# The scan of a state-space layer: splitting weights and summing squares on GpSimd instead of VectorE

## The chip, the cores and the metric

The program runs on one core of a Trainium2 chip. A core has a matrix engine (TensorE, PE in the rows), three engines for elementwise work (VectorE or DVE, ScalarE or ACT, GpSimd or POOL), and SyncE (SP), which here only issues transfers between HBM and the on-chip memory SBUF. Matmul results land in PSUM, which GpSimd cannot read. Each engine works off its own list of instructions strictly in order and waits for the others by semaphores. The metric is the device time of one execution in microseconds (us), lower is better.

## The reference, cut to what matters

```python
def reference(x, ...):
    x = first_block(x, ...)      # layer 1: RG-LRU and latent attention; layer 2: a state-space layer (SSD)
    return second_block(x, ...)  # short convolution, stick-breaking attention, MLP, gate

def _ssd_layer(x, w_in, conv_w, ...):            # layer 2, the one that the change touches
    z, xbc, dt = split(x @ w_in)                 # 1024 rows of sequence, 2048 + 3072 + 32 columns
    xs, bm, cm = split(silu(causal_conv(xbc)))   # 32 heads of 64; 4 groups with a state of 128
    for c in range(8):                           # chunks of 128 rows, one after the other
        decay = exp(cs_l - cs_s) where l >= s else 0       # cs: cumulative sum of dt * a
        y_diag = ((C_c @ B_c.T) * decay) @ (xs * dt)
        y_off  = (C_c @ state) * exp(cs)
        state  = state * exp(cs_end) + B_c.T @ (xs * dt * exp(cs_end - cs))
    y = (y_diag + y_off + d_skip * xs) * silu(z)
    y = y * rsqrt(mean(y * y over each group of 512 channels) + 1e-6)
    return (y * norm_w) @ w_out
...
```

Everything is float32.

## The kernel before, in words

Activations lie transposed in SBUF, channels on the 128 partitions and the sequence of 1024 along the free dimension. To keep float32 accuracy in a faster matmul format, each operand is split into a leading part (`hi`, rounded by ScalarE in a copy) and a trailing part (`lo`, the difference, made by the helper `lo` in line 260). `mm3` (lines 189, 193 and 194) then issues three matmuls for each product: hi·hi, lo·hi and hi·lo.

`weights` streams a weight block: for each four tiles of 128x128 it issues a DMA into `wr` (L179), ScalarE rounds it into `wh` (L180), and an engine subtracts to give `wl` (L260). Each of the three names has three buffers, so TensorE is fed two blocks ahead at most. The engine that makes `wl` is `self.weng`: GpSimd at the start, VectorE from the head of `phase_b` on, GpSimd again from `finish_b` on.

`phase_b` is layer 2. Its loop goes through 32 steps `(u, c)`: `u` is one of eight half groups of four heads, `c` one of four pairs of chunks. `stage1` loads the decay table into `L` (one buffer; L907), ScalarE turns it into exponentials (L911, L913), VectorE masks it (L916), and both operands `Xf` and `L` are split into `Xh`, `Xl`, `Lh`, `Ll`; it also advances the state (`hs`, `hh`, `hl`). `stage2` multiplies (`poff`, `pd` in the PSUM names `u` and `w`), adds up on VectorE in `et` (L971 to L988), multiplies by the gate in `zt` (L991), squares on ScalarE (L997) and adds the squares into `acc2` (L999, L1002). After two chunk pairs of a group's second half, a matmul with ones (L1007) sums `acc2` over the partitions, ScalarE takes the root and SyncE stores the row `rsd` (L1009). Between the steps, projections for later steps are slipped in (`conv_silu`, `proj_z`), and when these are used up, parts of the output projection (`part`), for which `y_act` loads the normalised `y` into the buffers `XH` and `XL` that the layer's input has left.

Where a group ends (every eighth step) the next group's `B` and `C` have to be prepared first (`prep_bc`), and only then can `stage1` go on.

The order on each engine isn't the order of the code: a scheduler sorts the recorded instructions by its own simulated times. So a small edit can move rows on every engine.

Of the kernel before, what the change touches and what calls it, by code (L numbers as in the profile page):

```python
# [12 lines left out]
A = mybir.AluOpType  # L13
# [36 lines left out]
class K:  # L50
# [38 lines left out]
    def v(self, name, i=0, n=1):  # L89
        o, _ = VEC[name]  # L90
        return self.vec[:, o + i:o + i + n]
# [5 lines left out]
    def P(self, nm, w=T):  # L97
        return self.ap.tile([128, w], F32, tag="P", bufs=self.ns, name=self.nm(nm))
# [650 lines left out]
    def phase_b(self):  # L749
        nc, v, P, R, cp, d = self.nc, self.v, self.P, self.R, self.cp, self.d  # L750
# [9 lines left out]


        first = self.first
        self.weng = nc.vector
        ps = first.pop(0)
        H = slice(0, 32)
        dt, e, cs = P("dt"), P("e"), P("cs")
# [53 lines left out]
        bc, xs, acc2 = {}, {}, {}  # L820
# [124 lines left out]
        def stage2(u, cpair):  # L945
            g, hg = divmod(u, 2)
            h0 = 8 * g + 4 * hg
            c0 = 2 * cpair
            th, tl, ch, cl, cbm = bc[g]
            xt = xs[u]  # L950
            Xh, Xl, Lh, Ll, prev = stg.pop((u, cpair))
            cols = slice(c0 * 128, c0 * 128 + 256)

            poff = self.u1()
            for c in range(2):
                if prev[c]:
                    hh, hl = prev[c]
                    s = slice((c0 + c) * 128, (c0 + c) * 128 + 128)
                    for p in range(2):
                        q = slice(p * 128, p * 128 + 128)  # L960
                        self.mm3(poff[:, c * 256 + p * 128:c * 256 + p * 128 + 128], (hh[:, q], hl[:, q]), (ch[:, s], cl[:, s]), True, True)
            et = self.E("et")
            ev = et.rearrange("p (c q l) -> p c q l", c=2, q=2)
            for j in range(2):
                for p in range(2):
                    nc.sync.dma_start(ev[64 * j:64 * j + 64, :, p, :], ecd[c0:c0 + 2, h0 + 2 * p + j, :].partition_broadcast(64))
            zt = self.E("zt")
            zv = zt.rearrange("p (q x) -> p q x", q=2)
            nc.sync.dma_start(zv, self.zd[u * 256:u * 256 + 256, cols].rearrange("(q p) x -> p q x", q=2))
            if c0:  # L970
                nc.vector.tensor_tensor(et, et, poff, op=A.mult)  # L971
            else:
                nc.vector.memset(et[:, 0:256], 0.0)
                nc.vector.tensor_tensor(et[:, 256:], et[:, 256:], poff[:, 256:], op=A.mult)
            for p in range(2):
                nc.vector.scalar_tensor_tensor(ev[:, :, p, :], xt[p][:, cols].rearrange("p (c l) -> p c l", c=2), v("d_skip", 4 * g + 2 * hg + p),
                                               ev[:, :, p, :], op0=A.mult, op1=A.add)

            for c in range(2):
                pd = self.u1()  # L980
                for p in range(2):
                    q = slice(c * 256 + p * 128, c * 256 + p * 128 + 128)
                    s = slice(c * HN + p * 256, c * HN + p * 256 + 256)
                    self.mm3(pd[:, p * 256:p * 256 + 256], (Xh[:, q], Xl[:, q]), (Lh[:, s], Ll[:, s]), True, True)
                pv = pd.rearrange("p (q j l) -> p q j l", q=2, j=2)
                for j in range(2):
                    r = slice(64 * j, 64 * j + 64)
                    nc.vector.tensor_tensor(ev[r, c], ev[r, c], pv[r, :, j, :], op=A.add)  # L988
            for p in range(2):
                z = zv[:, p, :].rearrange("p (c l) -> p c l", c=2)  # L990
                nc.vector.scalar_tensor_tensor(z, ev[:, :, p, :], 0.5, z, op0=A.mult, op1=A.mult)  # L991
            nc.sync.dma_start(self.yd[u * 256:u * 256 + 256, cols].rearrange("(q p) x -> p q x", q=2), zv)

            if g not in acc2:
                acc2[g] = P("acc2")
            sq = et
            nc.scalar.activation(sq, zt, AF.Square)  # L997
            if hg == 0:
                nc.vector.tensor_tensor(acc2[g][:, cols], sq[:, 0:256], sq[:, 256:], op=A.add)  # L999
            else:  # L1000
                for p in range(2):
                    nc.vector.tensor_tensor(acc2[g][:, cols], acc2[g][:, cols], sq[:, p * 256:p * 256 + 256], op=A.add)  # L1002
                if cpair % 2:
                    n = cpair // 2
                    s = slice(n * HN, n * HN + HN)
                    ps = self.u1()
                    nc.tensor.matmul(ps, self.ones, acc2[g][:, s], start=True, stop=True)  # L1007
                    self.rstd_from(acc2[g][:, s], ps, 1.0 / 512, 1e-6)
                    nc.sync.dma_start(self.rsd[g:g + 1, s], acc2[g][0:1, s])  # L1009
# [36 lines left out]
        for j, (u, c) in enumerate(steps):  # L1046
            last = c == 3 and u % 2
            if j + 1 < len(steps) and not last:
                stage1(*steps[j + 1])
            stage2(u, c)  # L1050
            if c == 2 and u % 2 and u < 7:
                load_bc(u // 2 + 1)
            if last and u < 7:
                prep_bc(u // 2 + 1)
                stage1(*steps[j + 1])
            if act:
                left = len(steps) - j
                for i in range(-(-len(parts) // left)):
                    part(parts.pop(0))
            elif u < 7:  # L1060
                project(PATTERN[j % len(PATTERN)])
                if not any(queue.values()):
                    for k in range(8):
                        act.append(self.y_act(k, self.XH[k], self.XL[k]))
# [864 lines left out]
```

## Time and profile before

| | us |
|---|---|
| median of 3 runs | 2759.99 |
| lowest, highest run | 2750.53, 2760.86 |
| the profiled execution's own time | 2749.49 |
| its span (first to last instruction) | 2747.7 |
| TensorE, VectorE, ScalarE, GpSimd busy | 2590.2, 1933.3, 1438.8, 655.1 |

The mean granted clock of TensorE is 0.975 of full speed. Busy times of different engines overlap, so they don't add up to the span; what counts in a stretch is which engine the others wait for. `phase_b` and the head of `finish_b` lie at 546 to 1276 us.

### The profile page before, as it was taken

What the parts mean: (1) busy time and instruction counts of PE and PEld (TensorE: products, weight loads), DVE (VectorE), ACT (ScalarE), POOL (GpSimd) and SP (SyncE); (2) the same over time, 40 slices, a digit from 0 to 9 for tenths busy, and PEclk for the clock granted to TensorE, in tenths of its full rate; (3) what the DMA queues carried; (4) which work ended last, traced back from release to release, by engine and by line L of the source; (5) the groups of instructions that cost most, each with busy time, mean ns of one, the idle gap of its engine ahead of it and who ended that gap; (6) DMA issues with size and microseconds to landing.
All of it is one profiled execution on the core that took longest, in us unless ns stands there. A gap on an engine that the chain in (4) does not pass through costs nothing. (4 is left out here: it accounts for less than half of the span.)

```text
span 2747.7 us, 34501 instructions
## 1 busy us (share of the span) xinstructions
PE 2590.2 (94%) x12000; PEld 2077.2 (76%) x12000; DVE 1933.3 (70%) x2754; ACT 1438.8 (52%) x2447; POOL 655.1 (24%) x467
## 2 busy tenths in 40 slices
PE   8999999999989899789989999998899999999997
PEld 6777887787877788677767776766688888887786
DVE  5683766769978698785575215889696666777577
ACT  5553754656656555543463224665665455443465
POOL 2642754400000000004455324566300000000024
PEclk9999999999999999889999999999999999999999
DMA  4444533443434344366443334543454446977324
GB/s 128 159 159 142 139 93 108 151 133 115 139 103 134 113 125 138 94 217 221 141 133 92 125 130 123 159 118 98 161 207 148 148 152 222 336 245 238 120 72 152
DMA packets 214419, 407.14 MB, mean 148 GB/s; under 512 B 22636, under 2 KB 61548, under 8 KB 214244
## 3 DMA queue, kind: packets, MB, share of 16 engines
q1 hardware_dynamic: 214244, 404.93, 45.9%
q8 instruction: 94, 1.54, 0.2%
q14 instruction: 81, 0.66, 0.1%
HBM read 297.35 MB, written 107.50 MB: 147 GB/s over the span
## 5 line engine op out<-in xcount | busy, mean ns | idle before, releaser
L260 POOL TENSOR_TENSOR wl<-wr,wh 128x512 fp32r<-128x512 f32 (+2 forms) x262 | 371.5, 1422 | 1158.4 <-ACT wh L180 1105.3
L189 PE MATMUL g<-XH,wh 128*128 128x512 f32 x1296 | 525.3, 406 | 23.8 <-ACT xc L812 10.3
L193 PE MATMUL g<-XL,wh 128*128 128x512 f32 x1296 | 523.7, 404 | 4.6 <-DVE XL L746 2.4
L194 PE MATMUL g<-XH,wl 128*128 128x512 f32 x1296 | 521.1, 402 | 4.7 <-POOL wl L260 4.7
L180 ACT CAST wh<-wr 128x512 fp32r<-128x512 f32 (+2 forms) x367 | 221.0, 604 | 395.5 <-PE g L193 164.8
L189 PEld LDWEIGHTS g<-XH,wh 128*128 128x128 f32 x1296 | 248.3, 192 | 85.1 <-ACT xc L812 11.3
L193 PEld LDWEIGHTS g<-XL,wh 128*128 128x128 f32 x1296 | 248.2, 192 | 65.4 <-DVE XL L260 4.4
L194 PEld LDWEIGHTS g<-XH,wl 128*128 128x128 f32 x1296 | 248.1, 191 | 64.8 <-POOL wl L260 6.3
L260 DVE TENSOR_TENSOR wl<-wr,wh 128x512 fp32r<-128x512 f32 (+1 forms) x198 | 133.0, 683 | 75.4 <-ACT wh L1531 45.0
L260 POOL TENSOR_TENSOR yl<-yl,yh 128x1024 fp32r<-128x1024 f32 x4 | 9.6, 2400 | 715.0 <-ACT yh L1075 712.3
L193 PE MATMUL m<-XL,XH 128*128 128x512 f32 x368 | 144.8, 393 | 5.5 <-DVE XL L260 5.5
L189 PE MATMUL m<-XH,XH 128*128 128x512 f32 x368 | 143.7, 392 | 0.0
L194 PE MATMUL m<-XH,XL 128*128 128x512 f32 x368 | 143.6, 392 | 0.0
L911 ACT ACTIVATE L<-L,tm 128x128 f32<-128x128 f32 x256 | 78.8, 389 | 122.4 <-DMA L<-csd 116.4
L194 PE MATMUL t<-XH,wl 128*128 128x512 f32 (+1 forms) x328 | 129.4, 395 | 1.3 <-POOL wl L260 1.2
L189 PE MATMUL t<-XH,wh 128*128 128x512 f32 (+1 forms) x328 | 128.2, 391 | 1.0 <-ACT wh L180 1.0
L193 PE MATMUL t<-XL,wh 128*128 128x512 f32 (+1 forms) x328 | 128.5, 392 | 0.0
L1615 ACT CAST XH<-a 128x1024 fp32r<-128x1024 f32 x46 | 48.2, 1049 | 134.6 <-PE m L193 109.3
L1283 DVE TENSOR_TENSOR_SCAN kp<-kp,zero 128x640 f32<-128x640 f32 (+5 forms) x64 | 107.0, 1693 | 5.5 <-ACT kp L1279 3.8
L1284 POOL TENSOR_TENSOR sg<-sg,kp 128x639 f32<-128x639 f32 (+5 forms) x64 | 91.3, 1436 | 75.5 <-DVE kp L1283 71.9
L577 ACT CAST XL<-t 128x512 fp32r<-128x512 f32 (+2 forms) x192 | 78.4, 426 | 46.1 <-DVE XL L260 21.2
L260 DVE TENSOR_TENSOR XL<-t,XL 128x512 fp32r<-128x512 f32 (+2 forms) x192 | 87.5, 472 | 14.8 <-ACT XL L577 14.0
(584 smaller groups left out, 6519.4 us busy)
## 6 DMA issues: line engine op xcount, KB each, us to landing
a<-w_down SPq DMA_DIRECT2D x64, 512.0 KB, 4.8
b<-hd SPq DMA_DIRECT2D x48, 512.0 KB, 5.7
wr<-wb_in SPq DMA_DIRECT2D x90, 256.0 KB, 2.7
wr<-wc_in SPq DMA_DIRECT2D x72, 256.0 KB, 2.8
L<-csd SPq DMA_DIRECT2D x32, 512.0 KB, 6.4
wr<-w_up SPq DMA_DIRECT2D x28, 512.0 KB, 4.9
wr<-wb_out SPq DMA_DIRECT2D x48, 256.0 KB, 4.7
hd<-t SPq DMA_DIRECT2D x48, 256.0 KB, 2.3
```

Source lines behind the costliest of these rows:

```text
L180: nc.scalar.copy(hi[:, :n], raw[:, :n])
L189: first = nc.tensor.matmul(ps, w[0], a[0], start=start, stop=False, skip_group_check=more)
L193: nc.tensor.matmul(ps, w[0], a[1], start=False, stop=False, skip_group_check=more)
L194: nc.tensor.matmul(ps, w[1], a[0], start=False, stop=stop, skip_group_check=more)
L260: eng.tensor_tensor(out, src, hi.bitcast(F32), op=A.subtract)
L577: nc.scalar.copy(th[:, y], ps[:, x])
L911: nc.scalar.activation(Lv[:, c, h, :], Lv[:, c, h, :], AF.Relu, scale=-1.0, bias=cs_t[:, (c0 + c) * 32 + h0 + h:(c0 + c) * 32 + h0 + h + 1])
L1283: nc.vector.tensor_tensor_scan(rv, rv, zero.to_broadcast([128, W]), 1.0, op0=A.mult, op1=A.add)
L1284: nc.gpsimd.tensor_tensor(sg[:, :W - 1], sg[:, :W - 1], kp[:, 1:W], op=A.mult)
L1615: nc.scalar.copy(hi, x)
```

## The change

`phase_b` no longer sets `self.weng` to VectorE. So all `wl` of the layer are made by GpSimd, and so are the eight `XL` that `y_act` makes with `self.weng` in the loop. The additions of squares into `acc2` are issued on GpSimd too.

```diff
@@ phase_b @@
         first = self.first
-        self.weng = nc.vector
         ps = first.pop(0)
...
@@ stage2 @@
             sq = et
             nc.scalar.activation(sq, zt, AF.Square)
             if hg == 0:
-                nc.vector.tensor_tensor(acc2[g][:, cols], sq[:, 0:256], sq[:, 256:], op=A.add)
+                nc.gpsimd.tensor_tensor(acc2[g][:, cols], sq[:, 0:256], sq[:, 256:], op=A.add)
             else:
                 for p in range(2):
-                    nc.vector.tensor_tensor(acc2[g][:, cols], acc2[g][:, cols], sq[:, p * 256:p * 256 + 256], op=A.add)
+                    nc.gpsimd.tensor_tensor(acc2[g][:, cols], acc2[g][:, cols], sq[:, p * 256:p * 256 + 256], op=A.add)
```

The lines behind the removed one have a number lower by one in the changed kernel (L916 is L915 there).

Three places show how the lists move. The first is VectorE where the second group begins, at the end of step `(2, 0)`; `et_6883` is that step's sum, `et_7053` the next step's, and `wl_7414` a weight block of a later projection. Before:

```order
737 L988 TENSOR_TENSOR et_6883<-et_6883,u_6894 64x256 x2
738 L935 TENSOR_TENSOR hs_6869<-hs_6869,t_6855 128x256
739 L934 TENSOR_TENSOR hs_7023<-hs_6869,dec 128x256
740 L260 TENSOR_TENSOR wl_7414<-wr_7412,wh_7413 128x512
741 L988 TENSOR_TENSOR et_6883<-et_6883,w_6903 64x256 x2
742 L916 TENSOR_TENSOR L_7002<-L_7002,cbm_6614 128x512 x2
```

The same place on VectorE in the changed kernel:

```order
690 L987 TENSOR_TENSOR et_6883<-et_6883,u_6894 64x256 x2
691 L934 TENSOR_TENSOR hs_6859<-hs_6859,t_6855 128x256
692 L933 TENSOR_TENSOR hs_6869<-hs_6859,dec 128x256
693 L260 TENSOR_TENSOR hl_6863<-hs_6859,hh_6862 128x256
694 L987 TENSOR_TENSOR et_6883<-et_6883,w_6903 64x256 x2
695 L990 SCALAR_TENSOR_TENSOR zt_6888<-et_6883,zt_6888 128x256 x2
```

The weight block that stood ahead of the second pair of additions into `et_6883` is gone from this list.

The second place is GpSimd at the same steps. Before, its list has no row between the last weight block of layer 1 and the head of `finish_b`. In the changed kernel:

```order
230 L260 TENSOR_TENSOR wl_7246<-wr_7244,wh_7245 128x512
231 L998 TENSOR_TENSOR acc_1188_6915<-et_6883 128x256
232 L260 TENSOR_TENSOR wl_7252<-wr_7250,wh_7251 128x512
233 L998 TENSOR_TENSOR acc_1188_6915<-et_7053 128x256
234 L260 TENSOR_TENSOR wl_7414<-wr_7412,wh_7413 128x512
235 L260 TENSOR_TENSOR wl_7420<-wr_7418,wh_7419 128x512
```

Weight blocks now stand behind sums of squares: `wl_7252` has to wait for the sum over `et_6883`.

The third place is where `y_act` fills `XH` and `XL` for the output projection, near the end of the loop; `yl` is the normalised `y`, `XL_72` to `XL_79` are the eight trailing parts. On VectorE before:

```order
1191 L1074 SCALAR_TENSOR_TENSOR yl_10499<-yl_10499,vec,rs_10487 128x1024
1192 L1074 SCALAR_TENSOR_TENSOR yl_10504<-yl_10504,vec,rs_10487 128x1024
1193 L260 TENSOR_TENSOR XL_73<-yl_10494,XH_65 128x1024
1194 L916 TENSOR_TENSOR L_10545<-L_10545,cbm_9630 128x512 x2
1195 L898 TENSOR_TENSOR Xf_10536<-t_10531,tm 128x256 x4
1196 L1074 SCALAR_TENSOR_TENSOR yl_10511<-yl_10511,vec,rs_10509 128x1024
1197 L260 TENSOR_TENSOR XL_74<-yl_10499,XH_66 128x1024
1198 L260 TENSOR_TENSOR XL_75<-yl_10504,XH_67 128x1024
```

On GpSimd in the changed kernel:

```order
298 L260 TENSOR_TENSOR XL_72<-yl_10489,XH_64 128x1024
299 L998 TENSOR_TENSOR acc_1684_9931<-et_10324 128x256
300 L260 TENSOR_TENSOR XL_73<-yl_10494,XH_65 128x1024
301 L260 TENSOR_TENSOR XL_74<-yl_10499,XH_66 128x1024
302 L260 TENSOR_TENSOR XL_75<-yl_10504,XH_67 128x1024
303 L260 TENSOR_TENSOR XL_76<-yl_10511,XH_68 128x1024
304 L260 TENSOR_TENSOR XL_77<-yl_10516,XH_69 128x1024
305 L260 TENSOR_TENSOR XL_78<-yl_10521,XH_70 128x1024
306 L260 TENSOR_TENSOR wl_10701<-wr_10699,wh_10700 128x512
307 L260 TENSOR_TENSOR XL_79<-yl_10526,XH_71 128x1024
```

Eight subtractions of 1024 columns have gone from VectorE's list to GpSimd's, one behind the other; the multiplications that make `yl` (L1074, L1073 in the changed kernel) stay on VectorE.

## Rows read from the trace of the kernel before

**Rows 1.** The page: the span.

```profile
span 2747.7 us, 34501 instructions
```

**Rows 2.** Busy us of each engine in stretches; PEclk is TensorE's granted clock.

```profile
core 0: us, PE busy (x) PEld busy (x) DVE busy (x) ACT busy (x) POOL busy (x), PEclk, DMA share, GB/s
546.00:1276.00 730.00, 676.70 (x3346) 560.42 (x3345) 599.08 (x1021) 405.00 (x686) 13.03 (x8) 0.95 0.45 137
...
780.00:800.00 20.00, 11.54 (x52) 9.54 (x51) 15.01 (x34) 10.59 (x19) 0.00 (x0) 0.69 0.33 84
...
1176.00:1206.00 30.00, 25.66 (x99) 19.93 (x100) 29.57 (x40) 16.39 (x24) 0.00 (x0) 0.81 0.74 240
```

**Rows 3.** Waits at 546 to 1270: total us, times, longest.

```profile
ACT et L997 <- DVE zt L991: 46.2, 16, 7.7
DVE wl L260 <- ACT wh L180: 30.2, 14, 4.7
...
PE t L189 <- ACT Xh L902: 16.0, 7, 5.3
```

**Rows 4.** Where a group begins, 786 to 791 us: start, duration, what.

```profile
786.50 2.44 ACT L911 ACTIVATE L<-L,tm 128x128 f32<-128x128 f32 x8 [5.48 <-DMA L<-csd]
788.85 0.60 ACT L180 CAST wh<-wr 128x512 fp32r<-128x512 f32 x1
...
789.49 0.69 DVE L260 TENSOR_TENSOR wl<-wr,wh 128x512 fp32r<-128x512 f32 x1 [4.71 <-ACT wh L180]
790.10 0.84 DVE L988 TENSOR_TENSOR et<-et,w 64x256 f32<-64x256 f32 x2
...
791.09 0.55 PE L189 MATMUL w<-Lh,Xh 128*128 128x256 f32 x1 [5.55 <-DVE et L988]
```

**Rows 5.** VectorE's forms, 546 to 1276 us: count, busy, mean ns, idle before.

```profile
L260 DVE TENSOR_TENSOR wl<-wr,wh 128x512 fp32r<-128x512 f32 x90 | 63.3, 704 | 30.4 <-ACT wh L180 30.2
L898 DVE TENSOR_TENSOR Xf<-t,tm 128x256 f32<-128x256 f32 x128 | 45.5, 415 | 4.3 <-PE t L891 4.0
L916 DVE TENSOR_TENSOR L<-L,cbm 128x512 f32<-128x512 f32 x64 | 41.6, 684 | 2.5 <-ACT L L913 2.1
...
L1002 DVE TENSOR_TENSOR acc<-acc,et 128x256 f32<-128x256 f32 x31 | 14.8, 478 | 2.0 <-ACT et L997 1.8
...
L260 DVE TENSOR_TENSOR XL<-yl,XH 128x1024 fp32r<-128x1024 f32 x8 | 9.6, 1216 | 0.0
...
L999 DVE TENSOR_TENSOR acc<-et 128x256 f32<-128x256 f32 x16 | 6.7, 416 | 0.0
...
L260 DVE TENSOR_TENSOR cl<-bc,ch 128x1024 fp32r<-128x1024 f32 x4 | 4.9, 1219 | 0.0
...
L974 DVE TENSOR_TENSOR et<-et,w 128x256 f32<-128x256 f32 x8 | 3.3, 407 | 0.0
```

**Rows 6.** Layer 1, 509 to 521 us: GpSimd's weight blocks: start, duration.

```profile
511.13 1.31 POOL L260 TENSOR_TENSOR wl<-wr,wh 128x512 fp32r<-128x512 f32 x1 [3.71 <-ACT wh L180]
513.89 1.30 POOL L260 TENSOR_TENSOR wl<-wr,wh 128x512 fp32r<-128x512 f32 x1 [1.45 <-ACT wh L180]
516.46 1.64 POOL L260 TENSOR_TENSOR wl<-wr,wh 128x512 fp32r<-128x512 f32 x1 [1.26 <-ACT wh L180]
519.03 1.36 POOL L260 TENSOR_TENSOR wl<-wr,wh 128x512 fp32r<-128x512 f32 x1 [0.93 <-ACT wh L180]
```

**Rows 7.** The same stretch on VectorE.

```profile
509.19 4.88 DVE L725 SCALAR_TENSOR_TENSOR t<-u,t 128x512 f32<-128x512 f32 x8 [1.22 <-PE u L723]
513.98 6.96 DVE L714 TENSOR_TENSOR a<-a,sq 128x512 f32<-128x512 f32 x6
```

**Rows 8.** GpSimd's other forms: in finish_b (page), and at the end (ns min/median/max).

```profile
L260 POOL TENSOR_TENSOR yl<-yl,yh 128x1024 fp32r<-128x1024 f32 x4 | 9.6, 2400 | 715.0 <-ACT yh L1075 712.3
...
L1775 POOL TENSOR_TENSOR o<-t,rst x6: 723/898/904, 2736.1 to 2740.3; 128x256 f32<-128x256 f32 x6
```

**Rows 9.** SyncE's own waits at 546 to 1270 us.

```profile
SPq L1009 <- ACT acc L294: 33.5, 7, 8.4
```

## The prediction

> **What bounds the kernel now.** The profiled execution took 2749.49 us, of which 2747.7 are its span [rows 1]. Every instruction that the change touches lies at 546 to 1276 us, so the table by stretches comes first [rows 2]. The reader is to see three numbers in its first row. TensorE is busy for 676.70 of 730 us, so 53 us pass without a matmul. Its granted clock is 0.95: with levels of 1.2 and 2.4 GHz that is about 73 us at the lower one (0.05 x 730 / 0.5), and half of these, 36 us, are lost. So nothing done in this stretch can win more than some 89 us, 3.2% of the whole. And VectorE is busy for 599.08 us, 82%, on an average; in some pieces it is full.
>
> Next the waits [rows 3]. TensorE's largest class of wait is for `Xh`, a rounding on ScalarE that follows VectorE's `Xf`: 16.0 us in seven pieces. VectorE for its part sat 30.2 us, fourteen times, in front of a `wl`, because ScalarE had not rounded that weight block yet. Whatever stood behind it in VectorE's list waited too. The longest of these is 4.7 us, and the timeline shows what it did [rows 4]: ScalarE waited for the table `L`, then worked through its eight activations from 786.50 on, rounded the weights at 788.85, VectorE's `wl` came at 789.49 after 4.71 us of nothing, and only then L988, which had all its data; TensorE, which needed the PSUM bank that L988 reads, stood for 5.55 us. That is a wait of the kind that this change removes.
>
> **What leaves VectorE.** 90 `wl` (63.3 us), the sums of squares in the stretch (14.8 + 6.7 us) and eight `XL` (9.6 us), together 94.4 us [rows 5], and with the `wl` the 30.2 us of waiting in front of them.
>
> **What GpSimd gets.** A `wl` alone takes 1.30 us there [rows 6]. An `XL` of 1024 columns takes 2.40, and a sum over 256 columns at least 0.72, going by the nearest form [rows 8]. So 90 x 1.30 + 48 x 0.72 + 8 x 2.40 = 171 us, on an engine that is busy for 13.03 us in this stretch [rows 2]. GpSimd's own time is covered. What it does to VectorE is not.
>
> **What GpSimd's work costs VectorE.** The trace of this stretch cannot show it, layer 1 can. From 509.19 on VectorE does eight multiplications, one operand in PSUM, in 4.88 us or 0.61 each, although a `wl` runs on GpSimd from 511.13 to 512.44 [rows 6, 7]. Then it does six additions with both operands in SBUF. At 0.61 they would take 3.66 us. They took 6.96, and three `wl` started in that time: 3.30 / 3 = 1.10 us for each. So a VectorE instruction with two SBUF operands stands still while GpSimd subtracts, one with a PSUM operand does not. The price of a `wl` for VectorE lies between 0 and 1.10 us. In the stretch, VectorE's remaining forms with both operands in SBUF (fourteen, from L916 down to `cl` in the list by cost) add up to about 346 us, those that read PSUM (twelve, from L898 down to L974) to about 179 [rows 5]: 66% against 34%. And VectorE is busy 82% of the time. I take 1.10 x 0.66 x 0.82 = 0.60 us, since neither end describes a mixed list. Scaled by length, a sum costs 0.33 and an `XL` 1.34 (without the 0.82, as VectorE is full there). Together 90 x 0.60 + 48 x 0.33 + 8 x 1.34 = 81 us. So VectorE's list gets shorter by 94 - 81 = 13 us, not by 94; the bounds are 94 shorter, and 50 longer if every instruction meets the full price (99 + 29 + 16 - 94).
>
> The Trainium skill, page "SBUF — State Buffer", section "Who interferes with whom", says that such a pair excludes each other and that whichever comes second is blocked until the first has finished. By that a `wl` would cost its whole 1.30 us where it bites, and the 54 us for the weights would be 64. The trace has 1.10 for it, so the measured price stands.
>
> **What reaches TensorE**, term by term.
>
> (a) The pause before 791.09. Without the `wl` L988 can start when its data are there, at about 784.8 (789.49 - 4.71). But then ScalarE is what is late: its activations end at about 788.9, and the projections that TensorE has next need PSUM that ScalarE empties. I take -4 of the 5.55 us. The bounds are 0, and -12 if the low clock of this piece (0.69 over 20 us, 6.2 us lost [rows 2]) goes with it.
>
> (b) The starts of groups. There TensorE lives from hand to mouth on the chain from the load of `L` over L911 and L916 to `Lh`, `Ll` and the next load, twice for each of four groups and once more at the end. In each pass a `wl` less saves 0.61 us; a `wl` on GpSimd that meets L916 or `Ll` costs 1.10, in two of three cases. That is 0.66 x 1.10 - 0.61 = +0.12, nine times: +1. Bounds -5.5 and +10 (always, never).
>
> (c) The eight `XL`. In 1176 to 1206 VectorE is full, 29.57 of 30 us [rows 2]. Without the `XL`, two `wl` and a sum some 18 us stay, of which 66%, 12 us, cannot run beside GpSimd. GpSimd needs 8 x 2.40 + 2 x 1.30 + 0.72 = 22.5 us for its list there. One after the other that is 34.5 us, against 30. I take +4, bounds 0 and +10.6 (all 18 us excluded).
>
> (d) The sums. A pair on GpSimd takes 1.44 us instead of about 0.83, and can stand behind a `wl` of 1.30. Behind the pair come the matmul with ones, the root, and the store for which SyncE waited 33.5 us in seven places [rows 9]; the load of `L` stands behind that store in SyncE's queue at the group ends. Four times 0.6: +2. Bounds 0 and +15 (eight times 1.9).
>
> The sum is -4 + 1 + 4 + 2 = +3 us, so 2752.5 for an execution like the profiled one. The four times shown fall into two near 2750 and two near 2760, and the median, 2759.99, is one of the upper two; with +3 it would be 2763. I take the middle of these, **2758 us**.
>
> **Rivals.** *VectorE's relief reaches TensorE (faster).* For it speaks that the waits in front of `wl` are 30.2 us and that VectorE is 82% busy; against it, that all fourteen are at most 4.7 us, and that the 13 us beside them are spread thin. The 43 us that VectorE would gain then reach TensorE by some 60%: -26, so 2732 us. It decides if a `wl` costs VectorE under 0.3 us, because they fall into its pauses or beside PSUM reads.
>
> *The exclusion at its full price (slower).* 90 `wl` at 1.10 us make VectorE's list 50 us longer, 20 with the waits removed, just where it is full; each new pause of TensorE can drop its clock, as the 0.69 and 0.81 beside today's pauses show [rows 2], which makes half as much again: +30, so 2788 us. It decides from about 0.9 us for each `wl`. The scheduler gives no protection that the trace shows: in layer 1 it let additions and `wl` collide. The rule of the Trainium skill that is named above leads here too, and a little further, to 1.30 us for each.
>
> *Weights late (slower).* On GpSimd a `wl` now stands behind sums that wait for ScalarE's square, which waited for `zt` 46.2 us in 16 places, 7.7 at most [rows 3]. Against it: TensorE has two blocks of 24 matmuls in hand, at 676.70 / 3346 = 0.20 us each 9.7 us [rows 2], and the worst case, 7.7 + 1.44 + 1.30 = 10.4, passes that only by a little. To reach 14 us most of the 32 steps would have to be late: 2772 us.
>
> That the change does less than its name says is visible before it runs: the eight `XL` go to GpSimd too. That is term (c), not a case of its own.
>
> **How the numbers follow.** 0.5%, about 14 us, is what a measurement of this kernel can tell from no change. I give the forecast (2744 to 2772 by itself) 0.48, the relief 0.22, the full price 0.26, late weights 0.04. So faster 0.22, same 0.48, slower 0.30. The range reaches into both rivals, 2732 to 2788, and holds the bounds of the terms except where several of them would come together.
>
> **What would show it.** Right: the wait for `wh` gone from VectorE and little of it on TensorE; VectorE's two-operand forms (L915, `Ll`, `Xl`, L814) with means 10 to 20% above those of before and the PSUM forms (L897, L987) unchanged; 171 us and somewhat more on GpSimd; TensorE's unbusy time at 546 to 1276 us between 45 and 65 us and its clock near 0.95; the pause at the start of the second group shorter by some 4 us. Wrong: if VectorE's two-operand forms are hardly longer, the price of 0.60 is too high and the kernel is faster; if TensorE waits for GpSimd's `wl` by more than a few us, or SyncE's waits for the root grow beyond 33.5 us by much, the terms (c) and (d) are too small. A new order that opens a pause of its own, which no row of before can show, would make the sum wrong at either side.

## The result, and the profile after

The changed kernel takes 2775.42 us (median of 13 executions, 2759.17 to 2777.1) against 2754.47 for the kernel before (13 executions, 2750.53 to 2762.69): a ratio of 1.0064, 95% interval 1.0051 to 1.0076, so about 17.6 us slower (the ratio goes by all executions; the two medians lie 21 us apart). The forecast was 2758 us and no change that can be measured.

First the span of the kernel after, from its page, which answers to [rows 1].

```profile
span 2772.8 us, 34625 instructions
```

Its table by stretches answers to [rows 2].

```profile
core 0: us, PE busy (x) PEld busy (x) DVE busy (x) ACT busy (x) POOL busy (x), PEclk, DMA share, GB/s
546.00:1276.00 730.00, 677.37 (x3342) 550.81 (x3341) 588.44 (x871) 404.32 (x688) 227.05 (x151) 0.97 0.44 136
1176.00:1206.00 30.00, 23.12 (x89) 18.59 (x89) 29.87 (x29) 11.79 (x14) 24.22 (x10) 0.79 0.48 171
```

In the whole stretch that the prediction looked at, little got worse: TensorE is busy as long as before, at a clock of 0.97 instead of 0.95. VectorE's list is 10.6 us shorter (forecast 13). The second row shows a place that did get worse: where seven of the eight `XL` and three other rows now fill 24.22 us of GpSimd's time, TensorE gets 23.12 us of work done instead of 25.66.

Next VectorE's and GpSimd's forms at 546 to 1276 us, which answer to [rows 5, 8] (line L915 here is L916 there, and so on).

```profile
L915 DVE TENSOR_TENSOR L<-L,cbm 128x512 f32<-128x512 f32 x64 | 61.5, 999 | 19.0 <-ACT L L912 13.2 <-DMA et<-ecd 5.8
L260 DVE TENSOR_TENSOR Ll<-L,Lh 128x1024 fp32r<-128x1024 f32 x32 | 46.1, 1440 | 7.4 <-ACT Lh L917 7.3
L897 DVE TENSOR_TENSOR Xf<-t,tm 128x256 f32<-128x256 f32 x128 | 45.4, 412 | 7.0 <-PE t L890 6.6
L814 DVE SCALAR_TENSOR_TENSOR xc<-xb,hw,xc 128x1022 f32<-128x1022 f32 x21 | 27.7, 1317 | 0.1
L987 DVE TENSOR_TENSOR et<-et,u 64x256 f32<-64x256 f32 x64 | 26.7, 417 | 1.1
L1073 DVE SCALAR_TENSOR_TENSOR yl<-yl,vec,rs 128x1024 f32<-128x1024 f32 x11 | 19.5, 1800 | 9.5 <-DMA yl<-yd 9.5
```

GpSimd's forms in the same stretch:

```profile
L260 POOL TENSOR_TENSOR wl<-wr,wh 128x512 fp32r<-128x512 f32 x94 | 154.5, 1645 | 348.6 <-ACT wh L180 304.6 <-PE t L194 19.5 <-DMA wr<-wb_in 9.2
L1001 POOL TENSOR_TENSOR acc<-acc,et 128x256 f32<-128x256 f32 x30 | 29.0, 968 | 71.8 <-ACT et L996 58.8 <-DVE xc L814 7.3 <-DVE cbm L859 4.6
L260 POOL TENSOR_TENSOR XL<-yl,XH 128x1024 fp32r<-128x1024 f32 x8 | 23.1, 2906 | 10.1 <-ACT XH L1074 5.7 <-DMA L<-csd 4.4
```

Forms with both operands in SBUF are longer (L915 999 ns, it was 684), those that read PSUM (L897, L987) are not. GpSimd pays as well: a `wl` takes 1.65 us there instead of 1.30, an `XL` 2.91 instead of 2.40.

The waits at 546 to 1276 us, which answer to [rows 3, 9]: VectorE's wait in front of `wl` is gone (it is GpSimd's now), TensorE hardly waits for GpSimd, and SyncE's wait for the root has not grown.

```profile
POOL wl L260 <- ACT wh L180: 304.6, 60, 11.9
...
PE t L189 <- ACT Xh L901: 15.0, 12, 3.7
...
PE g L193 <- POOL XL L260: 2.4, 2, 1.3
...
SPq L1008 <- ACT acc L294: 18.2, 6, 4.9
```

The pause of [rows 4] is gone too: at the start of the second group (774 to 792 us) TensorE's longest wait is 1.62 us.

```profile
779.64 0.39 PE L189 MATMUL t<-Xh,bth 128*128 128x256 f32 x1 [1.62 <-ACT Xh L901]
```

So most of what the prediction named as its signs is there, and the kernel is slower all the same. The place is found by cutting both executions at marks that TensorE passes in both: the first transposition of `xc`, the last product of the decay table with `x` in groups 1 to 3 and in each half of group 4, the middle of the matmuls on `yh` in `finish_b`, the last transposition of `vf` (the attention begins), the middle and the end of the attention's matmuls. Here are the two kernels on one chip, profiled once more for this (both in the list of experiments). First the kernel before: the stretches are groups 1, 2, 3, the halves of group 4, the head of `finish_b`, the rest up to the attention, its two halves, and all after it. The columns are those of the table by stretches above.

```profile
604.42:751.13 146.71, 138.00 (x713) 115.18 (x712) 129.96 (x229) 89.12 (x157) 0.00 (x0) 0.99 0.44 126
751.13:923.02 171.89, 158.45 (x792) 130.61 (x791) 137.60 (x244) 96.72 (x166) 0.00 (x0) 0.95 0.40 116
923.02:1093.01 169.99, 160.82 (x801) 132.72 (x801) 140.16 (x248) 96.21 (x165) 0.00 (x0) 0.96 0.44 124
1093.01:1175.11 82.10, 65.36 (x318) 56.03 (x317) 64.74 (x119) 43.75 (x76) 0.00 (x0) 0.85 0.36 101
1175.11:1277.36 102.25, 92.40 (x429) 74.85 (x430) 80.59 (x132) 42.99 (x71) 5.86 (x3) 0.93 0.71 230
1277.36:1344.39 67.03, 62.85 (x257) 49.49 (x257) 31.11 (x30) 21.25 (x33) 36.65 (x27) 0.95 0.53 162
1344.39:1701.53 357.14, 343.93 (x1426) 266.94 (x1424) 158.48 (x178) 143.90 (x221) 138.43 (x98) 0.97 0.37 118
1701.53:1814.74 113.21, 108.15 (x496) 75.40 (x494) 93.67 (x139) 72.05 (x161) 62.42 (x55) 0.88 0.48 138
1814.74:1966.03 151.29, 140.70 (x692) 104.78 (x692) 126.46 (x138) 92.85 (x186) 88.97 (x50) 0.94 0.39 112
1966.03:2749.81 783.78, 768.99 (x3325) 620.74 (x3324) 559.70 (x762) 397.78 (x617) 60.16 (x43) 0.99 0.55 187
```

The changed kernel between the same marks:

```profile
604.98:758.80 153.82, 136.41 (x679) 111.33 (x678) 130.37 (x199) 87.23 (x154) 37.66 (x27) 0.96 0.42 120
758.80:919.04 160.24, 152.91 (x787) 125.14 (x786) 134.13 (x212) 96.70 (x166) 44.87 (x33) 1.00 0.43 127
919.04:1084.67 165.63, 156.03 (x772) 127.67 (x772) 132.58 (x213) 95.56 (x164) 43.35 (x33) 0.96 0.43 121
1084.67:1172.01 87.34, 80.23 (x400) 65.44 (x399) 68.38 (x114) 45.69 (x81) 19.55 (x15) 0.94 0.42 113
1172.01:1280.65 108.64, 94.44 (x428) 76.61 (x427) 80.38 (x99) 43.29 (x71) 53.37 (x30) 0.92 0.63 214
1280.65:1351.63 70.98, 64.09 (x259) 49.53 (x259) 28.44 (x31) 20.84 (x33) 40.31 (x30) 0.95 0.53 163
1351.63:1707.98 356.35, 342.72 (x1425) 266.03 (x1424) 157.61 (x178) 143.79 (x221) 138.49 (x98) 0.98 0.37 119
1707.98:1831.99 124.01, 119.82 (x496) 83.71 (x494) 91.50 (x139) 72.94 (x161) 64.99 (x55) 0.79 0.43 125
1831.99:1983.45 151.46, 143.19 (x693) 105.40 (x692) 124.06 (x133) 91.49 (x184) 82.35 (x48) 0.93 0.38 112
1983.45:2771.24 787.79, 771.32 (x3323) 622.88 (x3322) 565.80 (x766) 398.03 (x619) 63.41 (x45) 0.99 0.55 186
```

The second number of a row is the length of the stage. The five stages of the scan take 672.9 us before and 675.7 after: +2.8, where +3 was forecast. In the two first profiles it is 667.5 and 670.5: +3.0. After the scan come +4.0 in the head of `finish_b`, -0.8 up to the attention, **+10.8 in the attention's first half**, at a clock of 0.79 instead of 0.88, +0.2 in its second half and +4.0 from there to TensorE's last matmul. (The two first profiles have +8.6, +3.4, +7.7, -0.9 and +3.8.) The attention's code and that behind it are the same in both kernels. So there were two questions: which of the moved parts costs what inside the scan, and why unchanged code behind it is slower.

### The profile page after: what moved, and what is told of

Same layout as the page of the kernel before. It is cut to its first block, busy times and chain, and to the rows that moved or that the text cites. A ratio compares the mean times of both kernels' runs of the same rounds, so it can differ in the third digit from the quotient of the medians.

```text
span 2772.8 us, 34625 instructions
## 1 busy us (share of the span) xinstructions
PE 2619.1 (94%) x12000; PEld 2086.6 (75%) x12000; DVE 1921.3 (69%) x2608; ACT 1437.4 (52%) x2447; POOL 878.8 (32%) x613
## 4 chain that ended last, share of the span: by engine, by line
PE 36%; DVE 7%; ACT 3%; DMA 3%; issue 2%; POOL 0%; SPq 0%; DVEq 0%; ACTq 0%; POOLq 0%
PE m L193 6%; PE m L189 6%; PE m L194 6%; PE g L193 2%; PE g L189 2%; PE g L194 2%; DVE XL L260 2%; DMA a<-w_down 2%; PE t L189 1%; PE t L193 1%; PE t L194 1%; PE s L1273 1%; PE t L574 1%; PE f L189 1%; PE f L193 1%
## 5 line engine op out<-in xcount | busy, mean ns | idle before, releaser
L260 POOL TENSOR_TENSOR wl<-wr,wh 128x512 fp32r<-128x512 f32 (+2 forms) x352 | 524.4, 1493 | 1508.8 <-ACT wh L180 1420.5
L260 DVE TENSOR_TENSOR wl<-wr,wh 128x512 fp32r<-128x512 f32 (+1 forms) x108 | 69.6, 666 | 46.7 <-ACT wh L1530 43.8
L634 POOL TENSOR_TENSOR pn<-pn,st 128x128 f32<-128x128 f32 (+3 forms) x64 | 73.6, 1160 | 59.9 <-DVE st L633 57.1
```

The source lines that it names most:

```text
L260: eng.tensor_tensor(out, src, hi.bitcast(F32), op=A.subtract)
L634: nc.gpsimd.tensor_tensor(p_, p_, r.to_broadcast([128, W]), op=A.mult)
```

## The experiments

Ratios are to the kernel before, executed on the same chip beside each group of runs; 0.001 is 2.76 us. Stage lengths come from one profiled execution each, cut at the marks above; it can be far from the program's median, so they tell less than the ratios (the profile of `XL` alone is the longest of that program's executions, that of weights and sums the shortest).

**One part of the change at a time.** Weights alone, weights and sums, XL alone, sums alone:

```diff
 # weights alone: the changed kernel, with
-        self.lo(self.weng, lo, y, hi)
+        self.lo(nc.vector if k < 8 else nc.gpsimd, lo, y, hi)
-                nc.gpsimd.tensor_tensor(acc2[g][:, cols], ...)     # both lines
+                nc.vector.tensor_tensor(acc2[g][:, cols], ...)
 # weights and sums: the first of these edits alone
 # XL alone: the kernel before, with nc.gpsimd for self.weng in y_act
 # sums alone: the kernel before, with nc.gpsimd in the two lines of acc2
```

> Only the weights' trailing parts go to GpSimd in the scan; the sums of squares and the eight XL stay on VectorE. The order of TensorE and VectorE from the attention of the second block on is then nearly that of the kernel before (6 rows of TensorE's differ, none of VectorE's). Theory 'scan': the engines of the scan carry the whole loss of about 17 us, the weights, as the longest of the three parts, most of it: 2763 to 2770 us, and TensorE idle at 546 to 1276 us over 60 us. Theory 'order': the scan itself costs 0 to 5 us and the rest is the lower clock that the changed order of the attention got at 1697 to 1735 us; with the order of before that piece is short again (7 to 14 us at the lower level) and the time is 2752 to 2759. Theory 'arrival': the long piece hangs on when TensorE arrives, not on the order behind it; it can come back here in some runs, which then stand 10 to 18 us above the others.

> The change without the eight XL, which stay on VectorE; weights and sums are on GpSimd. The later order is again nearly that of the kernel before. Theory 'scan': 2768 to 2772 us, since the XL were forecast at 4 us only. Theory 'order': 2754 to 2760 us, with at most 14 us of lower clock in the first 60 us of the attention. Theory 'arrival': as after in most runs, about 2772, with single runs near 2758.

> The kernel before with one edit: the eight XL that are made in the loop go to GpSimd; weights and sums stay on VectorE. Theory 'XL': eight subtractions of 2.9 us behind each other on GpSimd hold up the output projection that starts on them, so that the last half group of the scan takes 7 to 10 us more, and some 5 to 8 more are lost in the stages behind: ratio 1.004 to 1.008. Theory 'forecast': term (c), +4 us, ratio 1.0015. Theory 'order': the XL cost the scan little and the loss sits in the attention alone, whose order this edit changes in 1140 rows of TensorE: last half group within 3 us of before, ratio anywhere from 0.998 to 1.006.

> The kernel before with one edit: the sums of squares go to GpSimd; weights and XL stay on VectorE. The forecast's term (d) says +2 us (0 to +15), ratio 1.0005 to 1.001. The difference between the run with weights and sums and the run with the weights alone (0.9947 against 0.9987) says -11 us if the parts add up: ratio 0.996, with the gain between the fourth and the last half group.

| on GpSimd | ratio, 95% interval | scan, us | its last stage |
|---|---|---|---|
| nothing (before; two profiles) | 1 | 667.5, 672.9 | 100.3, 102.2 |
| weights | 0.9987, 0.9974 to 1.0001 | 675.5 | 105.4 |
| sums | 0.9964, 0.9948 to 0.9980 | 655.8 | 97.2 |
| XL | 1.0041, 1.0025 to 1.0057 | 687.2 | 113.9 |
| weights and sums | 0.9947, 0.9929 to 0.9965 | 663.4 | 98.5 |
| all three (after; two profiles) | 1.0064, 1.0051 to 1.0076 | 670.5, 675.7 | 107.4, 108.6 |

The theory that the weights carry the loss fell: they cost nothing. The sums on GpSimd are a gain of some 10 us, as expected from the difference of the two other runs, against the forecast's term (d). That run also has half of TensorE's rows in the scan in another place (1560 of 3045 by the traces), so whether the gain is the sums' own or their order's is not shown. `XL` alone moves 132 of them only. The eight `XL` alone cost 11 us (7 to 16), against the forecast's 4, and the change without them is *faster* than both kernels, than that of before by 15 us. A second measurement on another chip says the same:

> The change without the XL once more, on the chip of these runs. If its gain does not hang on the chip: ratio 0.993 to 0.9965.

It came to 0.9962 (0.9946 to 0.9977). The whole change is not the sum of its parts: 0.9987, 0.9964 and 1.0041 give 0.9992, and it is 1.0064. Half of the `XL`:

```diff
-        self.lo(self.weng, lo, y, hi)
+        self.lo(nc.vector if k < 8 and k % 2 == 0 else nc.gpsimd, lo, y, hi)
```

> Weights and sums on GpSimd, of the eight XL every second one (four), the others on VectorE. If each XL on GpSimd costs the same, half of the 33 us between the run without XL and the changed kernel: ratio 1.000 to 1.002. If the cost is the queue of eight behind each other (23 us at 2.9 us each, with the weights behind them), four side by side with VectorE's four cost little: ratio 0.995 to 0.998, and the last half group stays near 100 us instead of 108.

0.9996 (0.9983 to 1.0010), between the two ranges, its interval reaching into the first; and the scan's last stage takes 106.0 us, not near 100. So four `XL` already cost a good part of it, and the length of the queue is not the point. That each costs the same is likely, not shown.

**Both kernels again**, for the two tables above.

> The kernel before once more, profiled on the chip of these runs. Ratio 1.000. It tells how far two profiled executions of one program lie apart in each stage: 5 us in the scan and 4 us between scan and attention, if the run with the barrier is typical.

> The changed kernel once more, profiled on the chip of these runs. If the loss does not hang on the chip, ratio 1.005 to 1.0075 again. Theory 'arrival': with the long piece of low clock at the attention's start missing, some runs 14 us lower.

1.0004 (0.9987 to 1.0021) and 1.0066 (1.0049 to 1.0084). The loss doesn't hang on the chip.

**What GpSimd's work costs VectorE by itself.** Idle work beside VectorE's own `wl`, two operands and one:

```diff
             self.lo(eng, lo[:, :n], raw[:, :n], hi[:, :n])
+            if self.weng is nc.vector:
+                for q in (slice(c, c + 128) for c in range(0, 512, 128)):
+                    x = self.wp.tile([128, 128], F32, tag="wx", bufs=1, name=self.nm("wx"))
+                    nc.gpsimd.tensor_tensor(x, raw[:, q], hi[:, q].bitcast(F32), op=A.subtract)
+                    # or: nc.gpsimd.tensor_copy(x, raw[:, q])
```

> The kernel before plus idle work: after each wl that VectorE makes in the scan, GpSimd makes the same differences once more, in four pieces of 128 columns, into a tile that nothing reads. VectorE has no instruction less. Theory 'exclusion': VectorE's forms with both operands in SBUF get longer as in the changed kernel (L916 about 1000 ns instead of 684, Ll 1440 instead of 1219), the PSUM forms stay (L898 412, L988 416 ns); 90 times 0.60 to 0.85 us more on VectorE, 54 to 77 us, of which 60% reach TensorE: 30 to 46 us more in the scan. Rival: the longer instructions fall into VectorE's waits and TensorE loses under 8 us.

> As the run before, but GpSimd copies (one operand) instead of subtracting (two). All engines' other rows stand as in the kernel before, behind the scan too. If any work on GpSimd holds VectorE off, its forms with two SBUF operands get longer as there, and the scan by 20 us or more. If only GpSimd's instructions with two operands do, VectorE's forms keep their means within 2% and the ratio is 1.000 to 1.001.

1.021 (1.0185 to 1.0235) and 1.0019 (1.0006 to 1.0032). VectorE's and GpSimd's forms at 546 to 1276 us (lines stand 4 further here), with the subtractions:

```profile
L920 DVE TENSOR_TENSOR L<-L,cbm 128x512 f32<-128x512 f32 x62 | 45.4, 772 | 1.6 <-ACT L L917 1.5
L902 DVE TENSOR_TENSOR Xf<-t,tm 128x256 f32<-128x256 f32 x128 | 45.3, 415 | 3.2 <-PE t L895 3.0
...
L185 POOL TENSOR_TENSOR wx<-wr,wh 128x128 f32<-128x128 f32 x328 | 249.5, 761 | 467.3 <-issue 439.8 <-POOL wx L185 5.7 <-ACT wh L180 1.6
```

and with the copies:

```profile
L920 DVE TENSOR_TENSOR L<-L,cbm 128x512 f32<-128x512 f32 x64 | 42.6, 699 | 2.4 <-ACT L L917 1.9
...
L185 POOL COPY wx<-wr 128x128 f32<-128x128 f32 x360 | 186.6, 518 | 524.6 <-DMA wr<-wb_in 382.1 <-DMA wr<-wb_out 125.2
```

VectorE is held by the subtractions (L920 772 ns, 684 before and about 1000 expected; the PSUM form stays at 415), by the copies hardly (699, 2% more; the ratio lies a little above the expected 1.000 to 1.001). Added up over all forms, count times the difference of the means, VectorE's list gets 43 us longer by the subtractions and 10 by the copies; 54 to 77 were expected. The scan takes 708.7 us, 36 and 41 more than in the two profiles of before and within the 30 to 46 expected, but not by this alone, and the whole kernel loses 57: the subtractions read `wr` and `wh`, so the next loads wait for them as well (SyncE's queue waited 82.7 us for `wx` at 546 to 1316 us), and the scheduler has put TensorE's rows in another order in the scan and behind it. With the copies the order is that of before. So the two runs bear out the exclusion of two-operand work, and are no measure of its price for the time.

**Is it the order behind the scan?** The scheduler puts TensorE's rows from the attention on in another order in the changed kernel (in the traces, 817 of 4508 places there hold another row), though no line of it was edited. The runs with the weights alone and with weights and sums happen to keep the order of before but for 7 places. First, one barrier of all engines ahead of the attention, in both kernels.

```diff
+                self.tc.strict_bb_all_engine_barrier()
                 self.attend_c()
```

> The kernel before with one barrier of all engines between the second block's projections and its attention, so that both kernels enter the attention in the same manner. It is the base for the next run; the barrier itself is expected to cost 3 to 20 us. No theory sets a time for it.

> The changed kernel with the same barrier. Theory 'scan': 17 us above the kernel before with the barrier. Theory 'order': only what the stages up to the barrier lose, 5 to 13 us by the two traces (the shift is 6.7 us at 1259 us and 13.1 from 1405 on), and nothing behind it as long as the order behind the barrier stays close (its first 52 rows on TensorE are the same). Theory 'arrival': as 'order', since the barrier makes the arrival the same.

1.0064 (1.0044 to 1.0085) and 1.0103 (1.0081 to 1.0124). The difference, 0.0039, is 11 us, but 3 to 19 with both intervals, so it excludes neither the 5 to 13 of the theory of the order nor the 17 of the scan's. Besides, the barrier made new orders of its own, in the scan too (its five stages take 672.9 and 688.2 us), and the attention's first half took 134.2 and 129.3 us. This pair decides nothing. Then the order alone, and the sums with the order of before:

```diff
 # order run: the kernel before, in conv_act
-            for i in range(4):
+            for i in (2, 3, 0, 1) if n == 0 else range(4):
 # sums but one: the kernel before, both lines of acc2
+                (nc.vector if (u, cpair) == (4, 1) else nc.gpsimd).tensor_tensor(acc2[g][:, cols], ...)
```

> The kernel before with one edit far behind the scan: the four loads of the convolution's output that open the attention are issued in the order 2, 3, 0, 1. All engines' rows up to there are those of before; behind it 1150 rows of TensorE's stand elsewhere, in an order that lies within 119 rows of that of the run with the XL alone. No work is added or moved between engines. Theory 'order': the attention's first half takes 118 us instead of 113, with 45 us or more of lower clock there instead of 20 to 28, the rest 4 us more: 5 to 12 us in all, ratio 1.002 to 1.0045. Theory 'scan' (the later loss is an echo of the scan's end): ratio 0.9995 to 1.0005.

> The run with the sums alone on GpSimd, except that one of the 32 steps (u 4, c 2 of 8 chunks, the second pair) keeps its sum on VectorE. With that the order behind the scan is that of before but for 6 rows of TensorE. Theory 'order': the sums' gain in the scan (12 to 17 us) is no longer eaten by the attention (13 us) and the MLP (4 us): ratio 0.990 to 0.993. Theory 'scan': one sum in 32 changes nothing, ratio 0.996 as with all of them.

Both missed. The order run is 0.9995 (0.9981 to 1.0008): its profile has the longer first half of the attention (116.9 us) and 5 us more at the end, 3 us less in the second half, and the times show no loss at all. The sums but one are 0.9970 (0.9958 to 0.9982) instead of 0.990 to 0.993: the order was that of before, and the attention's first half took 122.0 us all the same.

So the last runs gave before, after and the change without `XL` one and the same later order, by the edit of the order run in each of them.

> The changed kernel with the edit of the order run (the four loads of the convolution's output in the order 2, 3, 0, 1). Its order behind the scan differs from that of the kernel before with the same edit in 30 rows of TensorE only, so the two differ by the scan and its immediate end. Theory 'order': what the changed kernel loses in the attention and the MLP (9 + 4 us) belongs to its order there; with the order of the order run, which cost nothing, only scan (+3 us) and the stage from the scan's end to the attention (+8) stay: ratio 1.003 to 1.0045. Theory 'scan': the loss belongs to the change wherever the later rows stand: 1.006 to 1.0075.

> The change without the XL, with the same edit of the loads; its order behind the scan differs from that of the order run in 8 rows. Theory 'order': the scan's gain of 6 to 9 us against the order run: ratio 0.996 to 0.9975. Theory 'scan': as without the edit, 0.994 to 0.9955.

1.0033 (1.0023 to 1.0044) and 0.9966 (0.9953 to 0.9979): both within what the theory of the order had set, and outside of the other's (the second's interval just touches it). With one later order, then, the change costs 1.0033 - 0.9995 = 0.0038, 10 us (5 to 15, the two intervals combined), of which the `XL` are 1.0033 - 0.9966 = 0.0067, 18 us (14 to 23), and weights and sums give back 8. The rest of the loss, 1.0064 - 1.0033 = 0.0031 or 9 us (4 to 13), goes by the times when the later order is another, while TensorE's order in the scan stays as it was. In the kernel before and in the change without `XL` the same edit gains nothing (0.9995; 0.9966 against 0.9962).

Two things keep this from being more than likely. The ratios compared come from different groups of runs, and the kernel before itself took 2754.76 us in one group and 2763.16 in the next on the same chip. And the profile does not show the 9 us: from the attention on, the changed kernel takes 1060.1 and 1063.3 us in its two profiles and 1059.6 with the edit, where the kernel before takes 1049.5 and 1048.3, and 1054.8 with the edit. The third pair of profiles also moves the loss: the five stages of the scan, in the same orders as in the two pairs above, take 665.4 us in the order run and 675.0 in the changed kernel with the same edit, +9.6 instead of +3.

What decides the attention's first half within one order stays open. The change without `XL` was profiled twice, the same program. The attention's first half took 112.52 us at a clock of 0.88 in the first profile:

```profile
1683.59:1796.11 112.52, 108.19 (x495) 75.47 (x494) 95.06 (x139) 71.88 (x161) 62.45 (x55) 0.88 0.49 138
```

and 121.97 us at 0.80 in the second:

```profile
1687.38:1809.35 121.97, 117.44 (x495) 82.72 (x494) 96.18 (x139) 72.48 (x162) 61.23 (x55) 0.80 0.44 128
```

In the first, TensorE ran at the lower level, 1.2 GHz, from 1677 to 1698 us, in the second from 1682 to 1685 and from 1692 to 1729. The second one's table in slices of 10 us shows a TensorE that is busy without a pause both while the clock is low and when it comes back, with the weights and the products of the attention in the same order as in the first:

```profile
1710.00:1720.00 10.00, 10.00 (x32) 7.15 (x32) 7.17 (x12) 5.11 (x13) 4.78 (x6) 0.50 0.34 99
...
1730.00:1740.00 10.00, 10.00 (x56) 7.87 (x54) 7.69 (x16) 5.24 (x13) 5.96 (x7) 1.00 0.39 128
```

So the order does not tell the two executions apart. Ahead of the lower level both have the same two pauses of TensorE, 0.78 and 1.29 us; why it lasted 21 us in one and 37 in the other stays open.

## Why the prediction was wrong, step by step

**The step that failed** is "Every instruction that the change touches lies at 546 to 1276 us". The rows lie there (all but one sum), but it cut the cost to that stretch as well. And in the stretch it mis-sized term (c), the `XL`: +4 us with a bound of +10.6, where they cost 18 (14 to 23) with the later order alike. Two things were not in the sum. The `XL` reach beyond the cut: the head of `finish_b`, which in fact ends at 1334 us in the first profile of before, takes 71.6, 71.0 and 69.7 us in the changed kernel's three profiles, against 63.0, 67.0 and 64.4. And the scheduler orders the whole program anew: 9 us by the times of the runs with one order, not found in the profiles. The prediction had said so of a "new order that opens a pause of its own", and given it neither a place nor a chance.

That the scan itself came out, +3 forecast and +3.0 and +2.8 in two pairs of profiles, is luck: the third pair has +9.6, and by the terms the errors cancel. What answers to (a) is some 7 us better than its term, what answers to (b) 5 to 7 worse, the last stage 2 to 3 worse than (c), and (d) has no stage of its own.

**The exclusion** was sized well on the whole. The same sum over forms (546 to 1300 us) gives 75 and 76 us for the two profiles after, 60 for the weights alone, 14 for the sums and 12 for the `XL`, against 54 + 16 + 11 = 81. Per `wl` that is 0.67 us, taken was 0.60, and not the 1.10 of the rival. The rule of the Trainium skill ("SBUF — State Buffer", "Who interferes with whom") holds here in its kind for the subtractions, and does not give the price: a `wl` of 1.65 us held VectorE for 0.67 on average, and the copies, which read SBUF too, held it hardly at all. That the two-operand forms get 10 to 20% longer was too even a guess: L814 3%, `Ll` 18%, L915 46%.

**(a)**, -4 us for the pause at the second group: its stage is 9.7 and 11.7 us shorter, with whatever else moved in that group. The bound of -12, with the low clock, was nearer: in the second pair the clock of the stage is 1.00 instead of 0.95.

**(b)**, +1 us for the starts of groups: the first group takes 2.3 and 7.1 us more, the first half of the fourth 5.2 in both pairs, the third 1.8 and 4.4 less. Together +6 to +8, though of whole stages and not of their starts alone, and more than was taken. The bound of +10 leaves out the 0.61 us saved in each pass; with it nine passes at full price make 9 x (1.10 - 0.61) = +4.4, and the measured is above that.

**(c)**, +4 us for the `XL`, was mis-sized and carries most of the cost. Against before the last stage of the scan is 7.1 and 6.4 us longer, but that has the sums' gain in it. Against the change without `XL`, three profiles of each, it is 11 longer (means 108.6 and 97.5) and the head of `finish_b` 5 (70.8 and 65.9), of 18 by the times. The two stages in the first profile of the run without `XL`, beside the rows of after:

```profile
1164.33:1262.78 98.45, 90.73 (x427) 73.63 (x427) 75.89 (x111) 44.12 (x72) 30.98 (x23) 0.95 0.70 242
1262.78:1328.57 65.79, 62.50 (x259) 49.42 (x259) 29.44 (x27) 21.25 (x33) 40.13 (x30) 0.97 0.55 169
```

98.45 and 65.79 us, against 108.64 and 70.98. The working counted GpSimd's 22.5 us once and let them start at once. In fact each `XL` takes 2.91 us there, and each `yl` that VectorE makes 1.80 us on average (L1073; 1.28 in the second profile of before). The second profile of after shows what that does to TensorE:

```profile
1189.94 5.80 DVE L1073 SCALAR_TENSOR_TENSOR yl<-yl,vec,rs 128x1024 f32<-128x1024 f32 x3
1194.50 9.36 POOL L260 TENSOR_TENSOR XL<-yl,XH 128x1024 fp32r<-128x1024 f32 x3 [2.24 <-ACT XH L1074]
1196.35 0.38 PE L189 MATMUL w<-Lh,Xh 128*128 128x256 f32 x1 [3.21 <-DVE et L973]
1199.00 5.14 DVE L975 SCALAR_TENSOR_TENSOR et<-xc,vec,et 128x256 f32<-128x256 f32 x2
1208.47 0.45 PE L189 MATMUL u<-ch,hh 128*128 128x128 f32 x1 [3.55 <-DVE et L987]
```

The same two L975 in the run without `XL`:

```profile
1193.36 0.87 DVE L975 SCALAR_TENSOR_TENSOR et<-xc,vec,et 128x256 f32<-128x256 f32 x2
```

So VectorE gains nothing by giving the `XL` away: from the first `yl` (1175.64 us) to the L987 behind the last (1207.48) its list takes 31.8 us; with the eight `XL` on VectorE and among these rows it takes 30.7. TensorE waits for `et` 3.21 and 3.55 us where it does not pause in the run without `XL`. Its order differs there too: between the transpositions of `xc` and the first of these products stand 12 matmuls of the output projection, in the run without `XL` 23. Over the stage 6.5 us more pass without a matmul, and the clock is 0.92 instead of 0.95; the term had neither.

**(d)**, +2 us for the sums (0 to +15), has the wrong sign: alone they gain 10 us, and beside the weights 7 to 11 (0.9987 against 0.9947 and 0.9962). The working looked only at what the root waits for, and that wait did not grow. What it left out may be the rows that stand behind a sum in VectorE's list: VectorE's wait in front of `wl`, at 546 to 1276 us, is half as long without the sums. First the kernel before in its second profile:

```profile
DVE wl L260 <- ACT wh L180: 30.6, 13, 4.9
```

then with the sums alone on GpSimd:

```profile
DVE wl L260 <- ACT wh L180: 15.2, 14, 3.0
```

By which way that reaches TensorE, and whether the new order in the scan has a part in it, was not taken apart.

**The rivals.** Some relief did reach TensorE, by (a) and with the sums, and the `XL` took it back. The exclusion at its full price and late weights did not happen: no row of TensorE's waits at 546 to 1276 us names GpSimd's `wl`. So what the forecast lacked are the `XL`, 18 us instead of 4, and likely 9 us of order.

## What to carry to other kernels

Moving several kinds of work at once can hide a gain behind a loss: here weights and sums were worth 8 to 15 us and eight instructions cost more than that, so try the parts alone before the whole is judged. When GpSimd takes work with two operands from VectorE, keep it away from where VectorE is full and TensorE lives on its results. That it is better placed where VectorE mostly reads PSUM or waits follows from the PSUM forms, which kept their length; no run here tried it. Where a scheduler sorts the whole program, a prediction needs a term for code that was not edited, and an experiment should give all its kernels the same order there.

## What the runs showed of the hardware

A copy of 128 columns on GpSimd, 360 times at 0.52 us, lengthened VectorE's list by 10 us; a subtraction of the same size, 328 times at 0.76 us, by 43. Where GpSimd subtracted 1024 columns, two VectorE instructions with both operands in SBUF took 5.14 us together that take 0.87 without. Both engines pay when they meet: GpSimd's `wl` went from 1.30 to 1.65 us, its subtraction of 1024 columns from 2.40 to 2.91. And one program's stage of 112.5 us took 122.0 in another execution, at a granted clock of 0.80 instead of 0.88, with the same pauses of TensorE ahead of the lower level: a difference of 10 us in one stage of two single profiles is not yet the change's.
